# Ten products of a zero tile ahead of the first projection, and the squares of the first norm queued behind the splits

## The chip, the cores and the metric

The kernel runs on one core of one Trainium2 chip. The number that counts is the device time of one execution, in microseconds (us). Before the change it is 896.19 us (median of 3 runs, 895.81 to 896.88).

The core has five engines that work from queues of their own: TensorE (PE in the profile, with its weight loads as PEld), VectorE (DVE), ScalarE (ACT), GpSimd (POOL) and SyncE (SP). An engine takes its instructions in the order of its queue and waits at each for what it needs.

## The reference

One hybrid decoder layer over 16 learned tokens and 512 given ones, width 1024, all in float32:

```
u    = rmsnorm(h, norm1_w)                  # h = [meta; x], 528 x 1024
proj = u @ w_in                             # into q, f, i, g, z, xbc, dt
h    = h + concat(hgrn2(...), mamba2(...)) @ w_out
h    = h + conv_glu_ffn(rmsnorm(h, norm2_w))
y    = rmsnorm(h, final_norm_w)[16:]
```

Only the beginning matters here: the first norm (mean of squares over the 1024 channels, then a reciprocal root), and the first projections of the normalised tokens.

## The kernel before

**Layout.** Tokens lie along the free axis (528 columns), channels along the 128 partitions, so the input is eight tiles `x0` to `x7` of 128 x 528. A product with the input projection goes over these eight k tiles. float32 accuracy comes from three products of a faster float32 form (`fp32r`): every operand is split into a high part (rounded by ScalarE) and a low part (the difference, by VectorE), and TensorE adds high x high, high x low and low x high. One output tile of 128 channels is thus 8 x 3 x 2 = 48 products, the last factor because the 528 columns are done as 272 and 256 (function `product`, line 190).

**The beginning** (lines 196 to 240). The loads of `x` and of the weights of the first two output tiles, named BT and CT in the code, come in quarters and alternate on SP's queue; `x0` and the parameters `pt` come over ScalarE's queue. For each k the high part `v_hi` (line 216, ScalarE) and the low part `v_lo` (line 217, VectorE) of `x` times the norm's weight are made, and for every second k the quarter splits of the two weight tiles (lines 160 and 161, forms of 128 x 256). BT and CT run side by side, 12 products for each k, on tokens that are not yet divided by the norm. The division comes after the product, when the bank is read.

**The first norm.** Each `x` is squared by ScalarE (line 227), VectorE adds the eight squares up (line 231), TensorE multiplies the sum by a matrix of ones (`psn`, line 242, plain float32), and ScalarE makes `rstd1` from it with Ln and Exp. VectorE then multiplies all eight `x` by it (`xn`, line 248), and the normalised tokens are split again (`u_hi`, `u_lo`), for all outputs but the first five. The first five are BT, CT and three tiles of x (here the first, second and third x product); they use `v_hi` and `v_lo` and their banks are read with `rstd1` (lines 277 to 280).

**Buffers.** Weights go through three raw buffers, three high and three low ones. A full split (128 x 1024) of a later tile waits until the product that used its buffer three tiles before has ended. Outputs go to two double banks (`banks2`), so a product waits until the one two before it has been read out, if the next buffer in turn is free. Small products use four single banks (`bank`).

**What sets the order.** The program is written in program order, but the order of the instructions in each engine's queue is set by a planner that models the run: among what is ready in its model it takes what has the highest priority. `first(n)` raises the priority of a block by n, `evac()` is `first(150000)`, and `first()` is `first(100000)`. The splits of the start are in `first(200000)`, the squares in `first(190000)`. `tc.issue_after(i)` makes the instructions of its block that run on the engine of `i` come behind `i` in that engine's queue; it sets no wait between engines.

Of the kernel before, what the change touches and what calls it, by code (L numbers as in the profile page):

```python
# [7 lines left out]
F32 = mybir.dt.float32  # L8
F32R = mybir.dt.float32r
I32 = mybir.dt.int32  # L10
AF = mybir.ActivationFunctionType
ALU = mybir.AluOpType
# [3 lines left out]
P = 128  # L16
# [16 lines left out]
C_N1 = 0  # L33
# [21 lines left out]
def tile_block(ctx: ExitStack, tc: tile.TileContext, xT, w_in, w_dt, w_out, w_up, w_down,  # L55
               par, consts, consti, out, dbg=None):
    nc = tc.nc
    V, A, G, PE = nc.vector, nc.scalar, nc.gpsimd, nc.tensor

    cp = ctx.enter_context(tc.tile_pool(name="cp", bufs=1))  # L60
# [7 lines left out]
    def slot(name, n=NT, dtype=F32, parts=P, tag="m"):  # L68
        return gp.tile([parts, n], dtype, tag=tag, name=name, bufs=TAGS[tag])

    def first(offset=100000):
        return tc.high_priority(offset=offset)
# [4 lines left out]
    def bank(name):  # L77
        return px.tile([P, 512], F32, tag="px", name=name)

    def banks2(name):  # L80
        return pj.tile([P, 1024], F32, tag="pj", name=name)
# [17 lines left out]
    def col(c):  # L99
        return pt[:, c:c + 1]  # L100
# [58 lines left out]
    def split_weights(raw, hi, lo, d, eng):  # L159
        A.activation(hi[:, d], raw[:, d], AF.Copy)  # L160
        eng.tensor_tensor(lo[:, d], raw[:, d], hi[:, d].bitcast(F32), ALU.subtract)  # L161
# [19 lines left out]
    def product(groups, xh, xl, t0, nk, k0=0):  # L181


        for k in range(len(xh)):
            first, last = k0 + k == 0, k0 + k == nk - 1
            for ps, (hi, lo) in groups:
                wh, wl = hi[:, k * P:(k + 1) * P], lo[:, k * P:(k + 1) * P]
                for w, x, s, e in ((wh, xh[k], first, False), (wh, xl[k], False, False), (wl, xh[k], False, last)):
                    for a0, a1 in ((t0, HALF), (HALF, NT)):
                        PE.matmul(ps[:, O + a0:O + a1], w, x[:, a0:a1], start=s, stop=e)  # L190
# [3 lines left out]
    vh, vl, xt, sqs = [], [], [], []  # L194
    starts = [raw_tiles(("in", j)) for j in (BT, CT)]
    wnext[0] = 2
    with first(200000):
        for k in range(0, KD, 2):
            d = slice(k * P, (k + 2) * P)
            for j, w, kx in ((BT, starts[0], k), (CT, starts[1], k + 1)):  # L200
                t = slot(f"x{kx}", tag="y")
                if kx == 0:
                    nc.scalar.dma_start(t[:], xT[:, kx, :])
                    nc.sync.dma_start(w[0][:, d], w_in[j][:, d])
                    nc.scalar.dma_start(pt[:], par)
                else:
                    nc.sync.dma_start(w[0][:, d], w_in[j][:, d])
                    nc.sync.dma_start(t[:], xT[:, kx, :])
                xt.append(t)
        for k in range(KD):  # L210
            if k % 2 == 0:
                for w in starts:
                    split_weights(*w, slice(k * P, (k + 2) * P), V)
            tag = "b0" if k < 4 else "b1"
            hi, lo = slot(f"v{k}_hi", dtype=F32R, tag=tag), slot(f"v{k}_lo", dtype=F32R, tag=tag)
            A.activation(hi[:], xt[k][:], AF.Copy, scale=col(C_N1 + k))
            V.scalar_tensor_tensor(lo[:], xt[k][:], col(C_N1 + k), hi[:].bitcast(F32), ALU.mult, ALU.subtract)
            vh.append(hi)
            vl.append(lo)
    with first(190000):  # L220
        wdt = slot("wdt", KD * 16)
        nc.sync.dma_start(wdt[:], w_dt)
        nc.sync.dma_start(cf[:], consts)
        acc = None
        for k in range(KD):
            sq = slot(f"sq{k}")
            A.activation(sq[:], xt[k][:], AF.Square)
            if acc is None:
                acc = sq
            else:  # L230
                V.tensor_tensor(acc[:], acc[:], sq[:], ALU.add)
    nc.sync.dma_start(maskA[:], consti)
    early = {BT: banks2("pj_b0"), CT: banks2("pj_c0")}
    used[0] = 2
    product([(early[BT], starts[0][1:]), (early[CT], starts[1][1:])], vh, vl, 0, KD)
    ahead(4)
# [2 lines left out]
    with first():  # L239
# [6 lines left out]
        for k in range(KD):  # L246
            t = slot(f"xn{k}")
            V.scalar_tensor_tensor(t[:], xt[k][:], col(C_N1 + k), rstd1[:], ALU.mult, ALU.mult)
            hi, lo = slot(f"u{k}_hi", dtype=F32R, tag="u"), slot(f"u{k}_lo", dtype=F32R, tag="u")
# [487 lines left out]
    for h in range(NH):  # L737
# [6 lines left out]
        hi, lo = slot(f"oa{h}_hi", dtype=F32R), slot(f"oa{h}_lo", dtype=F32R)  # L744
# [10 lines left out]
    for j, s in oorder:  # L755
# [11 lines left out]
        hi, lo = slot(f"u2h{j}", dtype=F32R, tag="u"), slot(f"u2l{j}", dtype=F32R, tag="u")  # L767
# [38 lines left out]
    for j in range(KF):  # L806
# [5 lines left out]
        hi, lo = slot(f"ac{j}_hi", 512, F32R, tag=tag[j]), slot(f"ac{j}_lo", 512, F32R, tag=tag[j])  # L812
# [141 lines left out]
```

## Time and profile before

| | |
|---|---|
| median of 3 runs | 896.19 us (895.81 to 896.88) |
| the profiled execution | 896.97 us, of which 895.3 us are the span from first to last instruction |
| PE busy | 875.2 us (98%), 6944 products |
| DVE busy | 553.8 us (62%) |
| ACT busy | 414.3 us (46%) |
| POOL busy | 23.9 us (3%) |
| mean DMA rate | 95 GB/s, 84.65 MB |

A row of the timeline gives the start, the duration, the engine (a "q" behind it is its queue issuing a transfer), the line of the kernel, the operation and the names of what it writes and reads; "x2" means that two of a kind were merged into a row. In brackets stands how long the engine had been idle and what ended the wait. TensorE's products overlap, so what one costs is read from the starts of two that follow one another and not from the duration.

### The profile page before, as it was taken

What the parts mean: (1) busy time and instruction counts of PE and PEld (TensorE: products, weight loads), DVE (VectorE), ACT (ScalarE), POOL (GpSimd) and SP (SyncE); (2) the same over time, 40 slices, a digit from 0 to 9 for tenths busy, and PEclk for the clock granted to TensorE, in tenths of its full rate; (3) what the DMA queues carried; (4) which work ended last, traced back from release to release, by engine and by line L of the source; (5) the groups of instructions that cost most, each with busy time, mean ns of one, the idle gap of its engine ahead of it and who ended that gap; (6) DMA issues with size and microseconds to landing.
All of it is one profiled execution on the core that took longest, in us unless ns stands there. A gap on an engine that the chain in (4) does not pass through costs nothing.

```text
span 895.3 us, 16372 instructions
## 1 busy us (share of the span) xinstructions
PE 875.2 (98%) x6944; PEld 834.4 (93%) x6944; DVE 553.8 (62%) x873; ACT 414.3 (46%) x632; POOL 23.9 (3%) x46
## 2 busy tenths in 40 slices
PE   7999999999999999999999999999999999999995
PEld 6998899999999999999999999999999999888885
DVE  6975968698776766454333367767766667423333
ACT  8629855865445444363222264444444444323220
POOL 1000000001000000000000000000000000000001
PEclk9999999999999999999999999999999999999997
DMA  7234332222221222245332323332333332233312
GB/s 247 88 100 162 120 97 71 72 51 69 72 56 63 95 72 72 84 142 154 94 96 94 95 86 97 86 91 92 94 96 94 95 95 89 83 91 103 89 42 94
DMA packets 29081, 84.65 MB, mean 95 GB/s; under 512 B 3128, under 2 KB 6712, under 8 KB 29008
## 3 DMA queue, kind: packets, MB, share of 16 engines
q1 hardware_dynamic: 26480, 80.02, 28.9%
q10 hardware_dynamic: 2528, 3.60, 1.4%
q8 instruction: 54, 0.88, 0.4%
q14 instruction: 19, 0.16, 0.1%
HBM read 81.45 MB, written 2.15 MB: 93 GB/s over the span
## 4 chain that ended last, share of the span: by engine, by line
PE 83%; DVE 4%; ACT 4%; DMA 1%; issue 1%; SPq 0%; DVEq 0%; ACTq 0%
PE pup L190 28%; PE pj L190 23%; PE pout L190 10%; PE pdn L823 4%; PE pdn L824 4%; PE pdn L825 4%; ACT L L467 1%; PE psu L441 1%; PE po L704 1%; PE po L703 1%; PE pa L686 1%; DMA ab<-acum_d 1%; DMA rs_d<-rh 1%; PE psx L429 1%; DVE ot L886 0%
## 5 line engine op out<-in xcount | busy, mean ns | idle before, releaser
L190 PE MATMUL pj<-u_hi,whi_in 128*128 128x272 f32 (+1 forms) x752 | 157.6, 289 | 2.4 <-ACT z L512 1.4
L190 PE MATMUL pj<-u_hi,wlo_in 128*128 128x272 f32 (+1 forms) x752 | 156.9, 287 | 0.0
L190 PE MATMUL pj<-u_lo,whi_in 128*128 128x272 f32 (+1 forms) x752 | 155.1, 286 | 0.0
L190 PE MATMUL pup<-u2h,wlo_up 128*128 128x258 f32 x704 | 141.6, 282 | 0.0
L190 PE MATMUL pup<-u2h,whi_up 128*128 128x258 f32 x704 | 140.7, 282 | 0.0
L190 PE MATMUL pup<-u2l,whi_up 128*128 128x258 f32 x704 | 140.6, 281 | 0.0
L190 PEld LDWEIGHTS pj<-u_hi,whi_in 128*128 128x128 f32 x752 | 115.8, 188 | 5.7 <-issue 2.5
L190 PEld LDWEIGHTS pj<-u_hi,wlo_in 128*128 128x128 f32 x752 | 116.6, 189 | 1.5 <-issue 1.2
L190 PEld LDWEIGHTS pj<-u_lo,whi_in 128*128 128x128 f32 x752 | 115.9, 188 | 1.6 <-issue 1.5
L190 PEld LDWEIGHTS pup<-u2h,wlo_up 128*128 128x128 f32 x704 | 108.0, 188 | 0.1
L190 PEld LDWEIGHTS pup<-u2l,whi_up 128*128 128x128 f32 x704 | 108.0, 189 | 0.0
L190 PEld LDWEIGHTS pup<-u2h,whi_up 128*128 128x128 f32 x704 | 107.6, 188 | 0.0
L161 DVE TENSOR_TENSOR wlo_in<-raw_in,whi_in 128x1024 fp32r<-128x1024 f32 (+1 forms) x58 | 64.3, 1109 | 36.5 <-ACT whi_in L160 35.9
L160 ACT ACTIVATE whi_in<-raw_in 128x1024 fp32r<-128x1024 f32 (+1 forms) x58 | 56.0, 965 | 54.6 <-PE pj L190 41.3
L825 PE MATMUL pdn<-ac_hi,wlo_dn 128*128 128x512 f32 (+1 forms) x198 | 73.0, 369 | 0.0
L823 PE MATMUL pdn<-ac_hi,whi_dn 128*128 128x512 f32 (+1 forms) x198 | 72.9, 368 | 0.0
L824 PE MATMUL pdn<-ac_lo,whi_dn 128*128 128x512 f32 (+1 forms) x198 | 72.8, 368 | 0.0
L160 ACT ACTIVATE whi_up<-raw_up 128x1024 fp32r<-128x1024 f32 x44 | 46.7, 1061 | 49.1 <-PE pup L190 32.5
L801 DVE SCALAR_TENSOR_TENSOR fc<-fr,pt,fc 128x512 f32<-128x512 f32 x88 | 65.9, 749 | 2.4 <-ACT fc L799 0.9
L161 DVE TENSOR_TENSOR wlo_up<-raw_up,whi_up 128x1024 fp32r<-128x1024 f32 x44 | 53.9, 1225 | 14.8 <-ACT whi_up L160 14.8
L161 DVE TENSOR_TENSOR wlo_dn<-raw_dn,whi_dn 128x1024 fp32r<-128x1024 f32 (+1 forms) x24 | 27.3, 1137 | 57.3 <-ACT whi_dn L160 57.3
L797 DVE TENSOR_TENSOR fr<-pup,rstd 128x514 f32<-128x514 f32 x44 | 30.5, 693 | 47.7 <-PE pup L190 43.7
(305 smaller groups left out, 1432.9 us busy)
## 6 DMA issues: line engine op xcount, KB each, us to landing
raw_in<-in_w_in_dram SPq DMA_DIRECT2D x50, 512.0 KB, 3.6
raw_up<-in_w_up_dram SPq DMA_DIRECT2D x44, 512.0 KB, 3.6
raw_out<-in_w_out_dram SPq DMA_DIRECT2D x16, 512.0 KB, 3.9
raw_dn<-in_w_down_dram SPq DMA_DIRECT2D x16, 512.0 KB, 3.6
ab<-acum_d SPq DMA_DIRECT2D x16, 264.0 KB, 4.8
raw_dn<-in_w_down_dram SPq DMA_DIRECT2D x8, 384.0 KB, 3.1
rb<-rs_d SPq DMA_DIRECT2D x8, 257.0 KB, 4.4
xr<-in_xT_dram ACTq DMA_DIRECT2D x8, 257.0 KB, 3.1
```

The lines of the kernel that those rows point to most:

```text
L160: A.activation(hi[:, d], raw[:, d], AF.Copy)
L161: eng.tensor_tensor(lo[:, d], raw[:, d], hi[:, d].bitcast(F32), ALU.subtract)
L190: PE.matmul(ps[:, O + a0:O + a1], w, x[:, a0:a1], start=s, stop=e)
L429: PE.transpose(psx[0:n, t * P:(t + 1) * P], xs[t][:, a0:a1], ident)
L441: PE.matmul(psu[:], btk[0:n, b * P:(b + 1) * P], xdc[b][0:n, :], start=True, stop=True)
L467: A.activation(L[:, a0:a1], ab[:, a0:a1], AF.Relu, bias=acm[:, b, h:h + 1], scale=-1.0)
L686: PE.matmul(pa[:, c:c + P], kA[:, META + c:META + c + P], qA[:, c:c + P], start=True, stop=True)
L797: V.tensor_tensor(r[:, T0:], ps[:, O + T0:O + NT], rstd2[:, T0:], ALU.mult)
L801: V.scalar_tensor_tensor(c[:], r[:, META - s:NT - s], col(C_FW + (2 - s) * 44 + j), c[:], ALU.mult, ALU.add)
L823: PE.matmul(ps, wh, xh, start=k0 + k == 0, stop=False)
L824: PE.matmul(ps, wh, xl, start=False, stop=False)
L825: PE.matmul(ps, wl, xh, start=False, stop=k0 + k == KF - 1)
```

## The change

Two things. The squares, their sum and the two loads in the same block get two `issue_after` edges: behind the last high part on ScalarE, behind the last low part on VectorE. And a block with the highest priority clears a tile of 128 x 256 in float32 on GpSimd and multiplies it by its own first 128 columns ten times, into a small bank that nobody reads.

```diff
-            A.activation(hi[:], xt[k][:], AF.Copy, scale=col(C_N1 + k))
-            V.scalar_tensor_tensor(lo[:], xt[k][:], col(C_N1 + k), hi[:].bitcast(F32), ALU.mult, ALU.subtract)
+            a_hi = A.activation(hi[:], xt[k][:], AF.Copy, scale=col(C_N1 + k))
+            a_lo = V.scalar_tensor_tensor(lo[:], xt[k][:], col(C_N1 + k), hi[:].bitcast(F32), ALU.mult, ALU.subtract)
             vh.append(hi)
             vl.append(lo)
-    with first(190000):
+            last_hi, last_lo = a_hi, a_lo
+    with first(190000), tc.issue_after(last_hi.ins), tc.issue_after(last_lo.ins):
         wdt = slot("wdt", KD * 16)
...
     early = {BT: banks2("pj_b0"), CT: banks2("pj_c0")}
+
+    with first(300000):
+        idle = cp.tile([P, 256], F32, name="idle")
+        G.memset(idle[:], 0.0)
+        pw = bank("pw")
+        for i in range(10):
+            PE.matmul(pw[:, 0:256], idle[:, 0:P], idle[:], start=True, stop=True)
     used[0] = 2
```

## Rows read from the trace of the kernel before

**Rows 1.** The page: span, busy time of the engines, and the head of the chain that ended last.

```profile
span 895.3 us, 16372 instructions
...
PE 875.2 (98%) x6944; PEld 834.4 (93%) x6944; DVE 553.8 (62%) x873; ACT 414.3 (46%) x632; POOL 23.9 (3%) x46
...
PE 83%; DVE 4%; ACT 4%; DMA 1%; issue 1%; SPq 0%; DVEq 0%; ACTq 0%
```

**Rows 2.** The waits of PE over the whole span: what waited, for whom, us in total, times, longest.

```profile
PE pj_b L190 <- ACT v_hi L216: 6.1, 1, 6.1
...
PE pj L190 <- ACT z L512: 1.4, 1, 1.4
```

**Rows 3.** Busy time by stage, the first 57 us and the 43 us behind them: length, then busy us (and instructions) of PE, PEld, DVE, ACT, POOL, granted clock, share of DMA, GB/s.

```profile
0.00:57.00 57.00, 49.23 (x378) 48.46 (x378) 49.72 (x87) 36.59 (x61) 2.24 (x21) 1.00 0.49 158
57.00:100.00 43.00, 43.00 (x358) 39.08 (x358) 29.08 (x57) 33.09 (x77) 0.65 (x2) 1.00 0.33 113
```

**Rows 4.** The timeline of PE: its first product, two pairs before 12 us and two after.

```profile
6.06 0.81 PE L190 MATMUL pj_b<-v_hi,whi_in 128*128 128x272 f32 x2 [6.06 <-ACT v_hi L216]
...
11.06 0.64 PE L190 MATMUL pj_c<-v_hi,wlo_in 128*128 128x272 f32 x2
...
11.50 0.64 PE L190 MATMUL pj_b<-v_hi,whi_in 128*128 128x272 f32 x2
...
12.23 0.40 PE L190 MATMUL pj_b<-v_lo,whi_in 128*128 128x272 f32 x2
...
12.48 0.41 PE L190 MATMUL pj_b<-v_hi,wlo_in 128*128 128x272 f32 x2
```

**Rows 5.** Busy time by stage again, for the 6 us from the first product on and the 6 us behind them (columns as in rows 3; the granted clock is the third number from the end).

```profile
6.05:12.05 6.00, 5.99 (x27) 6.00 (x28) 5.34 (x14) 5.48 (x13) 0.00 (x0) 1.00 1.03 358
12.05:18.00 5.95, 5.95 (x51) 5.95 (x50) 5.74 (x11) 5.95 (x12) 0.11 (x1) 1.00 0.52 162
```

**Rows 6.** The timeline of PE: the first norm's products of the ones, and near the end of the kernel one plain float32 product of 256 columns (which the profile counts as two) with the one that follows it.

```profile
20.09 1.05 PE L242 MATMUL psn<-sq,cf 128*128 128x272 f32 x4
...
874.89 0.59 PE L857 MATMUL psn<-facc,cf 128*128 128x256 f32 x2
...
875.32 0.28 PE L866 MATMUL psn<-cf,facc 128*128 128x1 f32 x2
```

**Rows 7.** The timeline of POOL: its first clearing of a full tile.

```profile
0.73 0.54 POOL L285 MEMSET wdp<- 128x528 f32 x1 [0.29 <-POOLq L942]
```

**Rows 8.** The timeline around 18 us: a low part on DVE, and the products before and after PE's wait for it.

```profile
17.69 0.77 DVE L217 SCALAR_TENSOR_TENSOR v_lo<-x,pt,v_hi 128x528 fp32r<-128x528 f32 x1
...
17.84 0.40 PE L190 MATMUL pj_c<-v_hi,whi_in 128*128 128x272 f32 x2
...
18.51 0.51 PE L190 MATMUL pj_b<-v_lo,whi_in 128*128 128x272 f32 x2 [0.27 <-DVE v_lo L217]
```

**Rows 9.** The timeline of ACT: five squares in a row, the eighth, the full split of the first x product's weights, the last high part, and the full split of the second x product's weights.

```profile
10.84 2.77 ACT L227 ACTIVATE sq<-x 128x528 f32<-128x528 f32 x5
...
15.82 0.63 ACT L227 ACTIVATE sq<-x 128x528 f32<-128x528 f32 x1
...
17.18 1.04 ACT L160 ACTIVATE whi_in<-raw_in 128x1024 fp32r<-128x1024 f32 x1
18.13 0.72 ACT L216 ACTIVATE v_hi<-x,pt 128x528 fp32r<-128x528 f32 x1
...
23.76 1.06 ACT L160 ACTIVATE whi_in<-raw_in 128x1024 fp32r<-128x1024 f32 x1
```

**Rows 10.** SP's queue: the issue of the last x and of the first raw tile behind it; and the time from issue to landing of the x tiles.

```profile
8.82 0.33 SPq L208 DMA_DIRECT2D x<-in_xT_dram  x1
...
10.26 0.43 SPq L169 DMA_DIRECT2D raw_in<-in_w_in_dram  x1
```

```profile
DMA to landing us min/median/max: 4.2/4.9/5.1
```

**Rows 11.** The timeline of DVE: the last low part, the eight xn behind the norm, the low half of the second x product's full split, the reading of the third x product's bank; and the stage from 40 to 50 us (columns as in rows 3).

```profile
20.13 0.76 DVE L217 SCALAR_TENSOR_TENSOR v_lo<-x,pt,v_hi 128x528 fp32r<-128x528 f32 x1
22.37 5.53 DVE L248 SCALAR_TENSOR_TENSOR xn<-x,pt,rstd 128x528 f32<-128x528 f32 x8 [1.48 <-ACT rstd L125]
...
28.43 1.22 DVE L161 TENSOR_TENSOR wlo_in<-raw_in,whi_in 128x1024 fp32r<-128x1024 f32 x1
...
48.52 0.69 DVE L280 TENSOR_TENSOR pr<-pj,rstd 128x528 f32<-128x528 f32 x1
```

```profile
40.00:50.00 10.00, 10.00 (x85) 9.83 (x84) 10.00 (x18) 2.23 (x3) 0.00 (x0) 1.00 0.46 147
```

**Rows 12.** The timeline from 49 to 57 us: the start of the first z product on PE, a full split and the copy of that product's bank on ACT, and the start of the second z product.

```profile
49.65 0.40 PE L190 MATMUL pj<-u_hi,whi_in 128*128 128x258 f32 x2
...
55.38 1.06 ACT L160 ACTIVATE whi_in<-raw_in 128x1024 fp32r<-128x1024 f32 x1 [2.96 <-issue]
56.34 0.58 ACT L512 ACTIVATE z<-pj 128x514 f32<-128x514 f32 x1
...
56.98 0.50 PE L190 MATMUL pj<-u_hi,whi_in 128*128 128x258 f32 x2 [1.45 <-ACT z L512]
```

**Rows 13.** The chain that ended last, two of its pieces: where it leaves PE after 160 us and where it is back on it.

```profile
160.65 1.35 ACT L L467 x5
...
210.25 6.28 PE pj L190 x50
```

## The prediction, made before the changed kernel ran

> **What bounds the kernel now.** I read the page first: TensorE is busy 875.2 of 895.3 us, and the chain that ended last runs through it for 83% [rows 1]. So time is won only where TensorE stands still or runs slowly, and a microsecond won early survives only if nothing later gives it back. The waits of TensorE over the whole trace come next [rows 2]: 6.1 us before its first product and 1.4 us for a bank near 56 us, both inside the stretch that the change touches. The stages [rows 3] show that VectorE is the second line: busy 49.7 of the first 57 us, with slack after that (29.1 of 43).
>
> Then the timeline of TensorE at the start [rows 4]. From 6.06 us, pairs of products of 272 and 256 columns begin 0.44 us apart (11.06, 11.50); from 12.23 they are 0.25 apart. 528 columns in 0.44 us is the pace of 1.2 GHz, in 0.245 us nearly that of 2.4 GHz. The granted clock is written as 1.00 in both stretches [rows 5], so this record does not show the low level and the pace does. TensorE ran 5.9 us without a pause before it rose. What the slow stretch cost: 27 products in 6.00 us [rows 5], which at 0.1225 us each (half of a 0.245 pair) take 3.3 us, so 2.7 us lost.
>
> **The change part by part.** The sum is made against the profiled execution: its time is 896.97 us, of which 895.3 are span. The median of the runs shown is 896.19, so 0.78 us comes off at the end.
>
> *The zero tile and its memset.* GpSimd clears 528 columns in 0.54 us from 0.73 us on [rows 7]; 256 columns are some 0.3 us. They delay the clearing of wdp, bS and the rest, which are used far later: nothing. TensorE can begin near 1.2 us (0.73 plus 0.3 and a hand-over; estimate).
>
> *The ten products.* They are plain float32, 256 columns. The one such product in the trace begins at 874.89 and its successor at 875.32: 0.43 us at full pace [rows 6]; the norm's products of 528 columns in all give the same rate. Ten are 4.3 us at full pace and 8.6 at half. No row shows when the clock rises under them. Bounds: if it rose at once they would end at 5.5 us, before the first token's high part at 6.05 [rows 4], and the front would win the whole 2.7; if it never rose during them they would end at 9.8, 3.7 us after the tokens were ready. I take the one row there is: 5.9 us of unbroken work, so a rise at 7.1. By then 6.9 are done (0.86 each), 3.1 remain at 0.43: the last ends at 8.4. With the low pace nearer to the measured ratio (0.44 to 0.245, so 0.77 each) it is 8.1. I take 8.3. The real products then start 2.2 us late but at full pace, against 2.7 lost before: 0.45 us gained.
>
> *The order of squares.* Now five squares run at 10.84 for 2.77 us, the eighth at 15.82, and the last high part starts only at 18.13 [rows 9]. TensorE feels this once: the product at 18.51 starts 0.67 after its neighbour at 17.84 and waits for the low part begun at 17.69 [rows 8]; 0.42 us is lost against a pitch of 0.245. That wait goes: starting at 8.3, TensorE needs k=7 only after seven groups of 12 products (10.3 us), at 18.6. The last x is issued at 8.82 and takes 4.9 us (median of its kind), landing near 13.7 [rows 10]; high and low parts end near 15.3. Front in all: 0.45 + 0.42, about 0.85 us.
>
> *What is late next: the first norm.* The squares now begin after the last high part, near 14.45, at 0.535 each (2.77 for five): done at 18.8, last add (0.70, as the form of the same size at 48.52 [rows 11]) at 19.5. TensorE ends the 96 products at 8.3 + 11.8 = 20.1, where psn also began before (20.09 [rows 6]). So the squares are covered by 0.6 us and the norm comes at the old time: VectorE's xn began 2.28 us after psn, at 22.37, having stood still since its low part begun at 20.13 [rows 11].
>
> *VectorE gives part of it back.* From 22.37 on it hardly rests (10.00 of 10 us from 40 to 50 [rows 11]). In its queue the reading of the third x product's bank stands at 48.52 and ends at 49.2 [rows 11]; the first z product, which takes that bank, began at 49.65 [rows 12]. The cover is 0.45 us. If TensorE is 0.85 earlier and VectorE not at all, 0.4 goes into a new wait there. Against that, the weights of the first output tile, BT, are free sooner (TensorE ends with them at 20.1, not near 24), so the full split that takes their buffer, the second x product's, can move: ScalarE did it at 23.76, VectorE at 28.43 for 1.2 us [rows 9, 11]. If VectorE's half falls into its pause before 22.37, VectorE is 1.1 us ahead and all 0.85 passes. Bounds: 0.45 and 0.85, below it if the squares are late (a rival). I take 0.8, since the pause is there and the split becomes ready inside it.
>
> *The wait of 1.45 us before 56.98* stays: ScalarE puts a full split (55.38, 1.06 us) ahead of the bank's copy (56.34), and both wait for the same product's end [rows 12]; it moves along with TensorE.
>
> *The rest* (bank pw, 1 KB of SBUF, edges on the two engines) costs nothing visible: the four small banks are first used at 20 us. The edges bind ScalarE and VectorE; the two loads in the block stay on SP's queue, where no instruction to wait for stands.
>
> Sum: 896.97 - 0.8 = 896.2, less 0.78 to the median: **895.4 us**.
>
> **The rivals.**
>
> A, the clock rises much sooner under unbroken products. If it rises after half of the row's time, 3 us, 3.5 products are slow, 6.5 take 2.8 us, the last ends at 7.0: front 1.75 + 0.42, 2.2 us; at the bound 3.1. VectorE must let it pass: with the early split it passes 0.45 + 1.1 = 1.55, and the full 2.2 only if its reading of the bank moves forward too. I take the 2.2: 896.97 - 2.2 - 0.78 = 894.0. For it: one row cannot say whether the moment of the rise hangs on the work before it alone. Against: that row says 5.9. The Trainium skill ("TensorE: Matmul & The Clock Gate", "Part 1") says the number of slow products in one kernel changes from run to run; no run here shows it, the three times being within 1.07 us. By it A would be as good as the row's figure.
>
> B, the norm comes later and nothing is won. If ScalarE still puts the first x product's full split before the last high part (17.18 before 18.13 [rows 9]), its raw tile issued at 10.26 lands at 14.5 (the shortest landing of an x, 4.2 [rows 10]), the split ends at 15.5, that high part at 16.2, the squares at 20.5, the last add at 21.2, and psn is 1.1 later than 20.1. VectorE's line is late by 1.1, less 0.45 of cover: 0.65 lost at the z product; 896.97 + 0.65 - 0.78 = 896.8. For it: the order of before has exactly that. Against: ScalarE has no squares to do while it waits, so the high part is ready first.
>
> C, slower: the clock does not rise under products of zeros. Place: 1.2 to 9.8 us. The ten take 8.6 us at half pace, the real ones start 3.7 us late and still pay the 2.7 that they pay now: 3.7 - 0.4 = 3.3 lost, 899.5. It decides if the ten keep 0.86 us each to the end. Against: no row ties the pace to the data.
>
> D, slower: the planner writes another order. The wait before 56.98 costs 1.45 us because a full split stands before a bank's copy [rows 12]; two more such places cost 2.9, less 0.8: 898.3. It decides from the second such place on. For it: everything after the start is planned with other times. Against: the planned order of the rest has no cause to be worse.
>
> That the change does not do what it says would be ten products behind the first token: not possible, as they wait for one memset.
>
> **How the numbers follow.** A measurement of this kernel tells about 0.2%, 1.8 us: below 894.4 is faster, above 898.0 slower. The forecast has 0.40 (894.6 to 896.3, all within), A 0.27 (faster; its price lies 0.4 beyond the edge), B 0.15 (within), C 0.07 and D 0.11 (slower; D by little). So faster 0.27, same 0.55, slower 0.18. The range from 892.8 to 898.4 leaves out the deep end of A, C and the deep half of D.
>
> **What would show it.** Right: products of the zero tile from about 1.2 us, ending at 8.1 to 8.4; the first pj_b product then at a pitch of 0.245 per pair; no wait for v_lo at 18; all squares after the eighth v_hi; psn near 20; the first z product near 48.8 instead of 49.65. A is shown by the ten ending before 7.5, B by psn or xn later than 21 and 23, C by 0.86 us for the tenth, D by new waits of TensorE after 25 us. The prediction is wrong if TensorE stands for psn, or if the first z product has not moved by 0.3 to 1.2 us, or if the gain there is lost again between 160 and 210 us, where the chain of waits leaves TensorE for ScalarE and VectorE [rows 13].

## The result, and the profile after

The changed kernel takes 898.36 us (median of 12 runs, 897.51 to 900.78) against 896.27 us of the kernel before in the same comparison (12 runs, 895.69 to 897.0): a ratio of 1.0024, 95% interval 1.0016 to 1.0031. It is slower by 2.1 us, where 895.4, a gain of 0.8, was forecast. The profiled execution took 898.59 us, of which 896.8 are span: 1.6 us over that of before.

Line numbers behind the new block are 8 higher than before. The page first, to be held against [rows 1]:

```profile
span 896.8 us, 16417 instructions
...
PE 879.7 (98%) x6964; PEld 837.3 (93%) x6964; DVE 555.6 (62%) x873; ACT 414.0 (46%) x632; POOL 24.1 (3%) x47
```

TensorE is busy for 4.5 us more: the ten products fill 6.6 us (1.10 to 7.68), and what they save of the slow stretch comes off. The span grew by 1.5. The waits of TensorE show what it met in place of the 6.1 us of [rows 2] (view and columns as there):

```profile
PE pj L190 <- ACT z L520: 1.4, 1, 1.4
PE pw L241 <- POOL idle L238: 1.1, 1, 1.1
...
PE pj L190 <- ACT pr L285: 1.0, 1, 1.0
...
PE pj L190 <- DVE dm L320: 0.4, 1, 0.4
PE pst L310 <- DVE dtx L306: 0.2, 1, 0.2
PE pj L190 <- DVE pr L288: 0.2, 1, 0.2
```

The wait for `v_lo` is gone and the one for `z` stayed, as forecast. New are 1.0 us for ScalarE's copy of the first bank (`pr`), and 0.8 us in three waits for VectorE. The timeline of TensorE puts them in place (to be held against [rows 4, 6, 12]):

```profile
1.10 6.93 PE L241 MATMUL pw<-idle 128*128 128x256 f32 x20 [1.10 <-POOL idle L238]
7.68 0.60 PE L190 MATMUL pj_b<-v_hi,whi_in 128*128 128x272 f32 x2
8.11 0.40 PE L190 MATMUL pj_c<-v_hi,whi_in 128*128 128x272 f32 x2
...
19.28 0.40 PE L190 MATMUL pj_c<-v_hi,wlo_in 128*128 128x272 f32 x2
20.69 0.51 PE L190 MATMUL pj<-v_hi,whi_in 128*128 128x272 f32 x2 [1.01 <-ACT pr L285]
...
23.71 1.05 PE L250 MATMUL psn<-sq,cf 128*128 128x272 f32 x4
...
50.70 0.47 PE L190 MATMUL pj<-u_hi,whi_in 128*128 128x258 f32 x2 [0.40 <-DVE dm L320]
...
58.07 0.51 PE L190 MATMUL pj<-u_hi,whi_in 128*128 128x258 f32 x2 [1.45 <-ACT z L520]
```

Each of the ten counts as two, so x20. They end when the real products begin, at 7.68, and from 8.11 on those run at the full pace (a pair every 0.245 us). BT and CT are done near 19.6, where before some of their products were left until 24. Then comes the turn: the queue goes on with the third tile (`pj` from 20.69, the first x product), which must wait for BT's bank, and only after 24 of its 48 products does `psn` come, at 23.71 instead of 20.09. ScalarE and VectorE in the same stretch (timelines, to be held against [rows 9, 11]):

```profile
13.68 4.37 ACT L228 ACTIVATE sq<-x 128x528 f32<-128x528 f32 x8
...
18.15 2.00 ACT L160 ACTIVATE whi_in<-raw_in 128x1024 fp32r<-128x1024 f32 x2
20.05 0.59 ACT L285 ACTIVATE pr<-pj_b 128x528 f32<-128x528 f32 x1
...
24.37 0.90 ACT L125 ACTIVATE rstd<-psn,eps 128x272 f32<-128x272 f32 x2 [2.28 <-PE psn L250]
```

```profile
14.87 3.96 DVE L232 TENSOR_TENSOR sq<-sq,sq 128x528 f32<-128x528 f32 x5 [0.30 <-ACT sq L228]
18.75 0.29 DVE L296 TENSOR_TENSOR wdp<-wdt,wdp 128x128 fp32r<-128x128 f32 x1
18.95 0.70 DVE L232 TENSOR_TENSOR sq<-sq,sq 128x528 f32<-128x528 f32 x1
19.57 1.22 DVE L161 TENSOR_TENSOR wlo_in<-raw_in,whi_in 128x1024 fp32r<-128x1024 f32 x1
20.71 0.70 DVE L232 TENSOR_TENSOR sq<-sq,sq 128x528 f32<-128x528 f32 x1
21.32 2.35 DVE L161 TENSOR_TENSOR wlo_in<-raw_in,whi_in 128x1024 fp32r<-128x1024 f32 x2
25.98 1.33 DVE L286 TENSOR_TENSOR pr<-pr,rstd 128x528 f32<-128x528 f32 x2 [2.30 <-ACT rstd L125]
...
49.87 0.69 DVE L288 TENSOR_TENSOR pr<-pj,rstd 128x528 f32<-128x528 f32 x1
```

All eight squares run in one go behind the last high part. The bank's copy at 20.05 stands behind two wide splits, and that is TensorE's 1.0 us. On VectorE five adds take 3.96 us, then half of `wdp` and a wide low part step in, and the last add ends at 21.4. ScalarE then stands idle for 2.28 us until `psn` is through, and VectorE for 2.30: its work that needs the norm begins at 25.98, where it began at 22.37, 3.61 us later. At the third x product's bank the delay is down to 1.35 us (49.87 against 48.52). What was caught up is seen when VectorE's instructions between the two points are grouped by line, before (22.37 to 48.52) and after (25.98 to 49.87):

```profile
L161 DVE TENSOR_TENSOR wlo_in<-raw_in,whi_in 128x1024 fp32r<-128x1024 f32 x5 | 6.1, 1211 | 0.0
```

```profile
L161 DVE TENSOR_TENSOR wlo_in<-raw_in,whi_in 128x1024 fp32r<-128x1024 f32 x3 | 3.6, 1205 | 0.0
```

Two wide low parts of 1.2 us went ahead of the norm, into VectorE's pause. The first z product waits for that bank and starts 1.05 us later than before (50.70 against 49.65 [rows 12]), the second 1.09 later. (The row names `dm`, the next instruction of VectorE; that the reading ends the wait is seen from its start, which is 0.83 us earlier, just as the product at 44.22, whose row names the reading, starts 0.84 us after one at 43.38.) From there the queues hold the same work in the same order, and most of the delay is carried on: the last product of the down projection ends 0.8 us later, the last VectorE instruction too. The span is 1.5 longer, and the missing 0.7 is in the last transfer of the output, in the view of the tile `out_dram`, before and after:

```profile
DMA to landing us min/median/max: 2.7/2.9/3.2
```

```profile
DMA to landing us min/median/max: 2.7/3.3/4.0
```

### The profile page after: what moved, and what is told of

Same layout as the page of the kernel before. It is cut to its first block, busy times and chain, and to the rows that moved or that the text cites. A ratio compares the mean times of both kernels' runs of the same rounds, so it can differ in the third digit from the quotient of the medians.

```text
span 896.8 us, 16417 instructions
## 1 busy us (share of the span) xinstructions
PE 879.7 (98%) x6964; PEld 837.3 (93%) x6964; DVE 555.6 (62%) x873; ACT 414.0 (46%) x632; POOL 24.1 (3%) x47
## 3 DMA queue, kind: packets, MB, share of 16 engines
HBM read 81.45 MB, written 2.15 MB: 93 GB/s over the span
## 4 chain that ended last, share of the span: by engine, by line
PE 82%; DVE 4%; ACT 4%; DMA 1%; issue 1%; SPq 0%; DVEq 0%; ACTq 0%
PE pup L190 28%; PE pj L190 23%; PE pout L190 10%; PE pdn L831 4%; PE pdn L832 4%; PE pdn L833 4%; ACT L L475 1%; PE psu L449 1%; PE po L712 1%; PE po L711 1%; PE pa L694 1%; DMA ab<-acum_d 1%; DMA rs_d<-rh 1%; PE psx L437 1%; DVE ot L894 0%
```

## The experiments

The theories at first: the edges do it, by setting `psn` behind the third tile so that VectorE's line is late (call it the late norm), or the ten products do, by holding the first real products back. The expectations call them Norm and Ten; a third, Squares, says that the late sum of squares costs, wherever `psn` stands. Times are compared with the kernel before on the same chip (896.1 to 896.5 us in all comparisons).

**The two halves apart.** e1 keeps the ten products and takes the edges out, e2 the reverse.

```diff
-    with first(190000), tc.issue_after(last_hi.ins), tc.issue_after(last_lo.ins):
+    with first(190000):
```

> The ten products alone, without the two edges: ScalarE's and VectorE's queues have the order of the kernel before, so the squares stand again ahead of the last high parts. Theory Norm (the loss comes from the norm's product psn standing 3.6 us later on TensorE, which makes VectorE's line late): psn stands where it stood before, at 20 us, TensorE spends its early lead waiting for high and low parts, and the time is that of before, ratio 0.999 to 1.001 (895.4 to 897.2). Theory Ten (the zero products themselves hold the first real products back, or leave the clock low in some runs): as slow as the change, ratio 1.0018 or more (898 us). Theory Squares (the edges make the sum of squares late, wherever psn stands): as before, 896.3.

```diff
-    with first(300000):
...
-            PE.matmul(pw[:, 0:256], idle[:, 0:P], idle[:], start=True, stop=True)
```

> The two edges alone, without the ten products. The planner puts 19 products of the third tile ahead of psn (24 in the change). Theory Norm: psn comes at 23 to 24 us, the first z product at 50.5 or later, and the time is as slow as the change or slower, since the slow first 6 us come back as well: 898 to 899.5. Theory Ten: the loss is gone, 895.8 to 896.5. Theory Squares: slow as the change, 898 to 899.

e1: 896.14 us (ratio 1.0000, 0.9991 to 1.0008). e2: 897.87 us (1.0020, 1.0012 to 1.0029). TensorE's timeline of e1, then of e2:

```profile
17.59 0.51 PE L190 MATMUL pj_b<-v_hi,whi_in 128*128 128x272 f32 x2 [0.33 <-ACT v_hi L216]
...
18.77 0.51 PE L190 MATMUL pj_b<-v_lo,whi_in 128*128 128x272 f32 x2 [0.43 <-DVE v_lo L217]
...
20.34 1.05 PE L250 MATMUL psn<-sq,cf 128*128 128x272 f32 x4
```

```profile
21.08 0.51 PE L190 MATMUL pj<-v_hi,whi_in 128*128 128x272 f32 x2 [0.68 <-ACT pr L279]
...
23.49 1.05 PE L244 MATMUL psn<-sq,cf 128*128 128x272 f32 x4
...
50.49 0.48 PE L190 MATMUL pj<-u_hi,whi_in 128*128 128x258 f32 x2 [0.33 <-DVE dm L314]
```

The edges alone carry the loss: the same late `psn`, the same wait at the z product, without any zero tile. The ten products alone change nothing; the lead that they give is spent waiting for the last high and low part, and `psn` starts where it did.

**`psn` ahead of the third tile.** e3 is the change, with the x products queued behind `psn`.

```diff
...
-                product([(ps, w)], vh, vl, t0, KD)
+                with tc.issue_after(psn.ins):
+                    product([(ps, w)], vh, vl, t0, KD)
```

> The change with one more edge: the products of the unscaled x tiles come behind psn in TensorE's queue, squares and adds as in the change. The plan of the later stages comes out otherwise as well (two more table loads on ScalarE). Theory Norm: psn begins when the last add ends, at 21.4 instead of 23.7, TensorE stands 1.9 us for it, the first z product begins near 49.5, and the time is 896 to 897. Theory Ten: still 898.4. Theory Squares: half of the loss stays, since the last add is still 2.3 later than in the kernel before: 897 to 897.8.

898.73 us (1.0026, 1.0016 to 1.0036): a miss, no better than the change. TensorE's timeline, and busy time by stage (columns as in rows 3, the granted clock third from the end):

```profile
22.12 1.16 PE L250 MATMUL psn<-sq,cf 128*128 128x272 f32 x4 [2.17 <-DVE sq L232]
...
24.15 0.43 PE L303 MATMUL psd<-v_hi,wdp 128*66 128x272 f32 x1
24.38 0.43 PE L304 MATMUL psd<-v_lo,wdp 128*66 128x272 f32 x1
```

```profile
22.00:24.00 2.00, 1.88 (x10) 1.70 (x11) 2.00 (x3) 1.82 (x5) 0.00 (x0) 0.87 0.72 227
24.00:26.00 2.00, 2.00 (x11) 2.00 (x10) 1.84 (x4) 0.46 (x1) 0.00 (x0) 0.50 0.64 188
```

TensorE stood 2.17 us for the last add, and behind that pause the clock fell to 0.50, its level of 1.2 GHz: `psd`'s products then start 0.23 us apart (24.15, 24.38), in the change 0.125. From 28 us on it is 1.00 again. The planner's order at least gave TensorE 24 products to do meanwhile. (The plan behind changed as well: the second z product was at 59.67 instead of 58.07.)

**The adds ahead of the wide splits.** e4 is e3 with VectorE's halves of the wide splits queued behind the last add (the edge binds the engine of the add alone).

```diff
-                V.tensor_tensor(acc[:], acc[:], sq[:], ALU.add)
+                last_add = V.tensor_tensor(acc[:], acc[:], sq[:], ALU.add)
...
-    ahead(4)
+    with tc.issue_after(last_add.ins):
+        ahead(4)
```

> As e3, and VectorE's two wide low halves come behind the last add of the squares; the plan behind 60 us is that of the change. Theory Norm: last add ends near 20.3, psn begins there, VectorE reads the banks 3 us earlier than in the change, the first z product begins at 48.5 to 49.3 (49.65 before, 50.70 in the change), and the time is 895.2 to 896.2, better than before. Theory Ten: 898.4 as the change. Theory Squares: 896.5 to 897, since the sum is still 1.2 later than before.

896.74 us (1.0007, 0.9999 to 1.0016): with these two orders the loss goes down to 0.5 us, and the last transfer still has the 0.7 of the change.

```profile
20.61 1.16 PE L251 MATMUL psn<-sq,cf 128*128 128x272 f32 x4 [0.39 <-DVE sq L232]
...
22.18 0.85 ACT L125 ACTIVATE rstd<-psn,eps 128x272 f32<-128x272 f32 x2
...
56.67 0.51 PE L190 MATMUL pj<-u_hi,whi_in 128*128 128x258 f32 x2 [1.44 <-ACT z L522]
```

`psn` still waits, 0.39 us, and Ln starts 1.6 us behind it, since a wide split and a bank's copy stand before it on ScalarE. The late norm shows by its repair: `psn` comes 3.1 us earlier than in the change, and the second z product at 56.67 instead of 58.07, earlier than before (56.98 [rows 12]). The time itself lies in the range that was named for Squares, not in that for Norm; at the second z product, though, nothing of the loss is left, and the 0.5 us have about the size of the late last transfer.

**Other places for the squares.** e5 has the ten products and free squares, but the wide splits behind the last parts. e6 has squares and adds behind the parts of the sixth token tile and the wide splits behind the last parts; e7 is e6 without the ten products, e8 with eight of them. The second half of the diff is that of e5, whose squares are as in e1; all of it is e6.

```diff
+            if k <= 5:
+                edge_hi, edge_lo = a_hi, a_lo
...
-    with first(190000), tc.issue_after(last_hi.ins), tc.issue_after(last_lo.ins):
+    with first(190000), tc.issue_after(edge_hi.ins), tc.issue_after(edge_lo.ins):
...
-    ahead(4)
+    with tc.issue_after(last_hi.ins), tc.issue_after(last_lo.ins):
+        ahead(4)
```

> The ten products, the squares free as in the kernel before, and only the wide splits of the next weights (ScalarE and VectorE) behind the last high and low part. Theory Norm, now with the second half that e1 showed (TensorE's lead is spent waiting for the parts of the last two k): the last high part comes near 17.2 and its low part near 19, TensorE still waits about 1 us for them, psn stands at 19.5 to 20, and the time is 895.4 to 896.2. Theory Squares: 895 to 896 as well. If the wide splits have no part in it: 896.1, as e1.

> The change with the edges on the sixth token tile's parts instead of the eighth's, and the wide splits behind the eighth's. The planner puts psn right behind the first two tiles' products and all of psd behind it. Theory Norm: TensorE runs from the ten products to psn without a wait of more than 0.3 us, psn begins at 19.5 to 20, the norm's result reaches VectorE near 22, the first z product begins near 48.8, and the time is 894.6 to 895.6, faster than before. Theory Squares (any edge on the squares costs): 896.5 or more.

> e6 without the ten products; ScalarE's and VectorE's queues are the same as in e6. Theory Norm: TensorE pays its slow first 6 us again, ends the two tiles near 20.5, psn follows there, and the time is 0.6 to 1.0 above e6: 895.4 to 896.4. If the ten products are worth nothing even under a good order: equal to e6 within 0.3.

> e6 with eight zero products instead of ten. They end near 6.9 to 7.3 instead of 7.7 to 8.2 if the clock has risen by then; the first real products start that much earlier. If TensorE's queue alone counts: 0.4 to 0.8 below e6. If the sum of squares (last add near 19.5) bounds psn: equal to e6 within 0.3, and TensorE stands for the add.

e5: 896.4 (0.9998, 0.9989 to 1.0006), as e1: the wide splits alone make no difference. e6: 897.38 (1.0010, 1.0001 to 1.0019), e7: 897.55 (1.0014, 1.0005 to 1.0023), e8: 897.71 (1.0014, 1.0005 to 1.0023). e6 was a miss, and its rows say why it wins nothing:

```profile
19.96 1.05 PE L253 MATMUL psn<-sq,cf 128*128 128x272 f32 x4
...
23.39 0.84 ACT L125 ACTIVATE rstd<-psn,eps 128x272 f32<-128x272 f32 x2
...
24.94 1.33 DVE L289 TENSOR_TENSOR pr<-pr,rstd 128x528 f32<-128x528 f32 x2 [0.69 <-ACT rstd L125]
```

`psn` is as early as before, but Ln comes 3.4 us behind it: two wide splits, the second of which waits 0.95 us for its weights to land, and two bank copies stand ahead of it on ScalarE. An early `psn` alone is no early norm. The rows do not say where e6 loses 1.1 us: its z products start where they did before (49.66 and 57.05), and its last transfer is not late. That is open. Nought, eight and ten products give the same time within 0.35 us.

**Less to read for VectorE.** e9 lets ScalarE copy the banks of the three x products as it does those of BT and CT; e10 is e13 (below) with the same copy.

```diff
-            if j in (BT, CT):
+            if j in (BT, CT, XT, XT + 1, XT + 2):
```

> The change, with the banks of the three x products copied out by ScalarE and divided by VectorE afterwards, as the first two tiles' are. VectorE's queue no longer holds a bank. If what the late norm costs is TensorE's waiting for VectorE to read banks (0.2 at 44 and 0.4 at 50.7 in the change, and the z product 1.05 late): these waits go, the first z product begins near 50.0, and the time is 897.3 to 897.9. If the loss sits elsewhere in VectorE's line (the dt chain, the scaled tokens): no gain, 898.2 or more.

> e4 with two more edits: the first half of psd stands ahead of psn, so that TensorE has 2 us of work while the squares are summed, and the banks of the three x products are copied out by ScalarE. If TensorE's queue is then without a wait up to the first z product: that product begins near 48.5 (49.65 before), and the time is 895.0 to 895.8 plus what e4 has at the end of the kernel (last transfer 4.2 instead of 3.5), so 895.3 to 896.3. If VectorE's line holds it all the same: 896.5 to 897.

904.69 us (1.0092, 1.0077 to 1.0108) and 899.11 us (1.0032, 1.0019 to 1.0044). Both inconclusive: the plan behind 58 us came out another way, with new waits of TensorE for VectorE of 2.9, 2.7 and 1.7 us in e9 and of 3.3 and 2.2 us in e10. In e10 the first z product was at 47.73, the earliest of all, and the time was lost all the same. Behind two of these pauses in each kernel the granted clock fell to 0.50 as well (in e9 behind 2.7 and 2.9 us, in e10 behind 2.2 and 3.3).

**The two kernels profiled again.**

> The change once more, for a second profile. If the last transfer's 4.3 us (3.5 in the kernel before) belongs to the program: 4.2 to 4.3 again; if to the execution: 3.5 as likely. The ten products end between 7.2 and 8.9, by when the clock rises; the first z product at 50.4 to 50.8, since VectorE's line sets it.

> The kernel before once more, for a second profile. Last transfer 3.5 if it belongs to the program. The pace of TensorE rises between 9.5 and 12.5, the first z product at 49.0 to 49.7.

897.79 and 896.67 us. In the change `psn` was at 23.83, the first z product at 50.83, in the kernel before at 19.99 and 49.54: the delay belongs to the programs, and so does that of the last transfer, which SyncE awaited for 4.2 and 3.5 us.

**Work for TensorE instead of a pause.** e13 is e4, with `wdp` made earlier and the first half of `psd` (16 products, which need no norm) put between BT and CT and `psn`. e14 is e13 with eight zero products; e15 is the change with six.

```diff
+    psd0_last = psd_half(0)
...
-            PE.matmul(p[:, 0:a1 - a0], ones, acc[:, a0:a1], start=True, stop=True)
+            with tc.issue_after(psd0_last.ins):
+                psn = PE.matmul(p[:, 0:a1 - a0], ones, acc[:, a0:a1], start=True, stop=True)
```

In e14, and with 6 in e15, the number of zero products:

```diff
-        for i in range(10):
+        for i in range(8):
```

> e4 with the first half of psd ahead of psn, and the banks read by VectorE as in the change (the plan behind 60 us is that of the change). TensorE has 2 us of work while the squares are summed, so it reaches the x products at 24.4 (25.5 in e4). If VectorE's reading of the third x product's bank (47.8 in e4) holds the z product: it begins near 48.6 to 49.0, and the time is 0.3 to 0.6 below e4: 896.1 to 896.5 with the last transfer of 4.2, 895.5 to 895.9 with 3.5. If TensorE's queue alone counts: 895.5 or less with 4.2.

> e13 with eight zero products. TensorE is some 0.6 earlier up to psn. If VectorE's line sets the z product: equal to e13 within 0.3. If TensorE's queue: 0.4 to 0.7 below e13.

> The change with six zero products, which end near 5.6 to 6.2, before the first high part. If VectorE's line (psn behind part of the third tile) sets the loss, the number of products has no part in it: the first z product at 50.3 to 50.8 and 898.0 to 898.6, as the change. If the ten products cost by holding the real ones back: 897.5 or less. Last transfer 4.2 if it comes with the edges behind the eighth parts.

e13: 894.52 us (0.9979, 0.9971 to 0.9988), e14: 894.88 us (0.9983, 0.9974 to 0.9992): both faster than either kernel. e13 came out where it was expected only if VectorE's line held nothing, though its z product does wait for VectorE; e16 to e18 below say why. e15: 899.51 us (1.0036, 1.0023 to 1.0049). Rows of e13, then of e15:

```profile
21.43 1.05 PE L268 MATMUL psn<-sq,cf 128*128 128x272 f32 x4
...
48.55 0.47 PE L190 MATMUL pj<-u_hi,whi_in 128*128 128x258 f32 x2 [0.32 <-DVE dm L334]
```

```profile
21.10 0.51 PE L190 MATMUL pj<-v_hi,whi_in 128*128 128x272 f32 x2 [2.60 <-ACT pr L285]
...
24.11 1.05 PE L250 MATMUL psn<-sq,cf 128*128 128x272 f32 x4
```

In e13 `psn` meets no wait, and the first z product is 2.15 us ahead of the change. In e15 the real products start at 6.23, 1.45 us ahead of the change, and TensorE waits 2.60 us for the bank instead of 1.01: the lead goes into that wait whole. (ScalarE and VectorE were some 0.4 us later in that execution, the first add at 15.29; the median is 1.1 us over that of the change, and the rest of this is open.)

**How much of e13 is the order.** Its chain of waits has one row that no order at the start should touch: 2060 products of the up projection took 243.77 us, as in e10 and e14, and 244.9 in the fourteen other profiles up to e15. The three share one moved line, by which the buffer of `wdp` is requested before those of `rstd1` and `u`, so that buffers can lie at other addresses (no trace shows addresses). e16 and e17 move that line alone, in the kernel before and in the change, with no other order of any queue; e18 gives e13 the old requests back.

```diff
+    wdp = slot("wdp", dtype=F32R, tag="pr")[:].rearrange("p (k m) -> p k m", k=KD)
     rstd1 = slot("rstd1", tag="rs")
...
-    wdp = slot("wdp", dtype=F32R, tag="pr")[:].rearrange("p (k m) -> p k m", k=KD)
```

> The kernel before with one line moved: the buffer of wdp is requested ahead of rstd1 and the u buffers, so that buffers lie at other addresses; the order of all instructions is that of before. In the three profiles with this line moved the stretch of 2060 up-projection products took 243.77 us, in all fourteen others 244.91 or 244.93. If the addresses do it: 243.8 there, first z product at 49.6 as before, and a time 1.1 us under before, near 895.2 (0.9987). If it is the order of the instructions in those kernels: 244.93 and 896.3.

> The change with the same line moved, orders those of the change. If the addresses do it: up-projection stretch 243.8, first z product near 50.7 as in the change, and a time near 897.1 (1.0010), 1.15 us under the change. If not: 898.3 (1.0024).

> The kernel of e13, with rstd1 and the first two u buffers requested ahead of wdp, so that the buffers lie as in before; same order of instructions as e13. If the addresses give 1.15 us of e13's 1.9: up-projection stretch 244.9, first z product at 48.55 as in e13, time near 895.6 (0.9992). If the whole gain of e13 comes from the order at the start: 894.5 (0.9979).

e16: 894.96 us (0.9985, 0.9976 to 0.9994). e17: 898.66 us (1.0027, 1.0017 to 1.0036). e18: 895.81 us (0.9992, 0.9983 to 1.0001). The row in the chains of e16, e17 and e13:

```profile
514.49 243.77 PE pup L190 x2060
```

```profile
515.93 244.91 PE pup L190 x2060
```

```profile
514.48 243.77 PE pup L190 x2060
```

So of the 1.9 us that e13 wins over the kernel before, some 0.7 may be the order at the start (e18: 895.81 against 896.48; its interval just includes no difference), and the greater part came with the moved line, which is worth 1.5 us to the kernel before by itself (896.48 - 894.96). Why it does nothing in the change (e17) is open; so addresses are not settled as the cause. The change and the kernel before have the same 244.9 in this row, so none of the loss of the change lies there.

## Why the prediction was wrong, point by point

**The ten products: right in kind.** They did raise the clock, and the real products began at 7.68 (8.3 said). Their prices, 0.86 and 0.43 us, were right; what was set too late is the rise of the clock (near 5.7 in the change, an estimate from the 6.6 us that the ten took at these prices; 7.1 was said), and its moment is not fixed: in the twelve profiles with ten of them the first real product starts between 6.84 and 8.25, and in the change itself at 7.68 and, in e11, 7.14. The Trainium skill ("TensorE: Matmul & The Clock Gate", "Part 1") says that the number of slow products changes from run to run; these runs agree. With the `v_lo` wait gone TensorE was done with BT and CT near 19.6, not 20.1. Rival C is refuted: ten products at half pace would have ended at 9.8. A was to be shown by an end before 7.5; e11 has that (real products from 7.14), and none of A's gain.

**The step that failed: "the squares are covered by 0.6 us and the norm comes at the old time".** It had two errors. The adds were counted as one, 0.70 us behind the last square. But each needs the sum before it, and five took 3.96 us, 0.79 each: from 14.87 on seven take until 20.4, already later than TensorE's 19.6, although the squares ended at 18.05 (18.8 said). Half of `wdp` and a wide low part between them made it 21.4. (e4, with only the half of `wdp` between, has `psn` at 20.61.) And `psn` was taken to follow the 96 products. With the adds so late, the planner put 24 products of the third tile ahead (none in e6, where the adds are earlier), and these wait for a bank whose copy stands behind two wide splits: 1.0 us of pause, 3.0 us of products. So `psn` came at 23.71 instead of 20.1, and VectorE's line started 3.61 us late.

**The cover of VectorE: right in kind.** The step said that the first z product hangs on the reading of the third x product's bank, with 0.45 us to spare. In all eleven profiles in which it waits (the change, e2, e6, e13 and e15 among them) it starts 0.83 or 0.84 us after that reading starts; before, 48.52 + 0.83 = 49.35 against 49.65, so 0.3 were to spare. The early wide splits that the step hoped for came too, two instead of one (2.26 us caught up). The rest, 1.35 less the 0.3, is the 1.05 us at the z product: the sum of the front was to be -0.8 there and was +1.05.

**Rival B** had this path, a norm too late that is paid at the z product, but not its size: it gave 1.1 us of lateness from a wide split ahead of the last high part, which did not happen, and 0.65 us of loss. **Rival D** named a new order of the planner as the way to lose; the new order is there, in one place at the start, and what it says of the rest is not: behind the first 58 us the queues are the same.

**Not foreseen: 0.7 us in the last transfer.** It goes with the program: present in the change, e2, e4, e11, e15 and e17, absent from the fourteen other profiles. In these six, and in none of the fourteen, a packet of 8 KB for the instruction queue (q14) falls into the transfer. The view of the DMA queues in the change, from the issue of the last output to its landing (891.8 to 895.8 us):

```profile
q14 instruction: 1, 0.01, 0.5%
...
out_dram<-ot ACTq DMA_DIRECT2D x1, 256.0 KB, 4.0
```

No run moved that packet, so that it causes the delay is likely and not shown.

**What the two account for.** In the mean of the two profiles of each kernel the second z product starts at 58.14 and 56.92: 1.2 us, and with the 0.7 it is 1.9 of the 2.1. The same sum gives e2 1.7 (1.6 measured) and e4 0.4 (0.5); it fails for e6 (0.1 against 1.1). A single execution can carry 0.7 more or less: in the last norm, from 887 to 890 us, the granted clock was 0.50 in the change, the kernel before and e12, and 0.81 in e11, where the four products `psr` took 0.71 us instead of 1.22 (in the change). So e11's span is only 1.0 over e12's.

**Where luck comes in.** The 898.36 lies just inside the stated range (to 898.4), but the range went that far for Rival D's sake; the forecast was a gain.

**The test named ahead** tells it: "the prediction is wrong if [...] the first z product has not moved by 0.3 to 1.2 us"; it moved 1.05 the other way.

## What to carry to other kernels

A head start on the busiest engine is worth only what the next engine's line lets through: ask first which wait that line ends, here the reading of one bank at 49 us, and what starts it. When a reduction is moved back in its engine's queue, count its dependent steps one by one and look where its consumer then stands in the other engine's queue. If that engine has to bridge a gap, give it work that does not need the result (e13's half of `psd`), for a pause of 2.2 us cost the pause and then the clock (e3).

## What the hardware showed that was not expected

- In e3 one pause of 2.17 us was followed by a granted clock of 0.50, and in e10 one of 2.16, while the 2.60 us of e15 and the 1.01 us of the change were not. The length of a pause alone does not decide. The stage behind e15's pause:

```profile
22.00:24.00 2.00, 2.00 (x19) 2.00 (x19) 2.00 (x2) 0.49 (x1) 0.00 (x0) 1.00 0.84 254
```

- The granted clock is given as 1.00 from 1 to 6 us of the change, while the zero products run at half pace (the six of e15 take from 1.10 to 6.23, 0.86 us each, against 0.43 in [rows 6]), as in the slow stretch of [rows 5]; in these views a low level at the start is seen from the pace only.
- An 8 KB packet for the instruction queue inside the last transfer of the output goes with a landing 0.7 us later in six of twenty profiles, and with none in the other fourteen.
- One moved request for a buffer, with the order of all queues unchanged, was worth 1.5 us in the kernel before, of them 1.16 in the 2060 products of the up projection, and nothing in the change. A gain of that size in a comparison of orders has to be looked for in a stretch that the order does not touch before it is put down to the order.
